# A hybrid encoder block on one core: x2 transposed and split once for both feed-forward chunks, and a planner with a larger reserve per hand-over

## The chip, the cores and the metric

The kernel runs on 1 core of one Trainium2 chip. Time is device microseconds of one execution, and the comparison is between medians of several executions. One execution was also recorded by the hardware profiler; its engines are PE (TensorE, with PEld for its weight loads), DVE (VectorE), ACT (ScalarE), POOL (GpSimd) and SP (SyncE, which issues the DMAs).

## The reference

One encoder layer on 256 tokens of width 2048, in float32, with one final RMSNorm:

```
x = x + W_out [ MLA(h) || DiffAttn(h) ],   h = RMSNorm(x)
x = x + CrossAttn(RMSNorm(x), RMSNorm(mem))        (256 memory tokens, 4 heads)
hf = rms_norm(x, g_ffn)                            # x * rsqrt(mean(x*x) + 1e-6) * g
x = x + (silu(hf @ w_gate) * (hf @ w_up)) @ w_down # w_gate, w_up: 2048 x 5632
return rms_norm(x, g_final)
```

The change is in the third line's `hf`, which the kernel calls x2, and in the first 512 of the 5632 hidden columns.

## The kernel before, in words

**Arithmetic.** TensorE multiplies float32r operands. A value v is held as two halves, h = the rounded copy (a CAST on ACT) and l = v - h (a TENSOR_TENSOR subtract on DVE); a product is three matmuls, h·h, h·l and l·h. `split_into` makes both halves, of weights and of activations alike, so each weight megabyte that arrives (`wraw`) costs ACT two casts and DVE two subtracts of 128x1024.

**Two forms of product.** `project` takes one 512-column chunk: for each of 16 K tiles, 2 token tiles, 3 matmuls of 128x512. `wide_project` takes 1024 columns as a sum over 8 K pairs. A pair of kind "P" is plain: 2 K tiles x 2 token tiles x 2 column halves x 3 = 24 matmuls. A pair of kind "W" uses Winograd's form of Strassen's 2x2 product: 7 block products x 3 = 21 matmuls, at the price of sums. The weights' sums (`tsum`) are one DVE add of 128x1024 and two of 128x512 per pair, and 3.5 instead of 2 subtracts of 1024 columns; the activations' sums are made once by `summed_pair` (4 adds of 128x128, and the forms' splits of 256, 256 and 512 columns). At the end of a wide product `leave` takes the four summed banks out of PSUM (1 ACT copy, 4 DVE operations of 128x512), and `join` adds the four plain banks (4 DVE operations).

**The feed-forward part.** Column block 0 (512 columns) is the narrow chunk, the other 5120 are five wide chunks. After the output projection of cross attention (`w_xo`, 4 column blocks `oc`), each block of x2 is added to the residual (`xres`), transposed on PE, multiplied by g_ffn (`x2T_f`) and split into `x2T`. The narrow chunk uses `x2T` without 1/rms in two `project` calls, gate and up, and multiplies by 1/rms (`rstdf`, tile `x2Tr`) afterwards. Between the two, `normalized_pairs` puts 1/rms into a row (`rb`, two transposes `rps`, `rrow`), multiplies the four `x2T_f` tiles of 128x1024 by it, and splits them a second time, into 4 plain pairs (`x2n`) and 4 summed ones (`forms`). Wide chunks use those. A wide chunk is a gate product, Silu on ACT, an up product, h = up * silu(gate) on DVE, transposes, `hT`, and after every one or two chunks a down product into `xres`.

**What sets the order.** Nothing is issued as it is written: class `Plan` records every operation with its needs and a cost in microseconds, and emits each engine's instructions in an order of its own. A first pass fixes the order of the matmuls; two more passes give each other operation a due time (`wanted`), going back from its readers, and each engine takes the earliest due among what can begin soon. Before the change the step from a reader to what it waits for is the operation's latency plus `HANDOVER` = 0.06 us. All instructions are issued by one recording helper, so they carry one line in the profile (L225 before, L227 in the change): groups are told apart by their tiles.

**Buffers that bind.** `wp` holds 3 raw weight tiles (`wraw`, 1 MB each) and 4 pairs of split halves (`wh`, `wl`). PSUM has 4 accumulator banks and 4 for everything else, and the two sets change places at the end of each wide product.

Of the kernel before, what the change touches and what calls it, by code (L numbers as in the profile page):

```python
# [178 lines left out]
class Plan:  # L179


    HANDOVER, CHOICE = 0.06, 0.3
    BEGUN = {"tensor": 0.6, "vector": 0.8, "scalar": 0.7, "sync": 0.7, "gpsimd": 0.3}

    def __init__(self, tc):
# [59 lines left out]
    def cost(self, engine, method, out, ins, kw):  # L245
        if method == "dma_start":
            size = max(x.cols() for x in out + ins) * 512
            return {"gpsimd": 0.55, "sync": 0.45, "scalar": 0.45}[engine], 2.0 + size / 375e3, size / 381e3
        n = max([x.cols() for x in out[:1]] + ([x.cols() for x in ins[:1]] if "reduce" in method else []))
        in_psum = bool(ins) and ins[0].tile.whole  # L250
        if engine == "tensor":
            t = 0.108 if method == "transpose" else 0.0134 + n / 2400
            return t, t + 0.14, 0.0
        if engine == "gpsimd":
            if method in ("memset", "affine_select", "tensor_copy"):
                t = 0.1 + n * 1.2e-3
            else:
                t = 0.59 if n == 1 else 0.7 if n == 2 else 1.0
            return t, t + 0.03, 0.0
        if engine == "vector":  # L260
            if n <= 16 and "reduce" not in method:
                t = 0.08
            elif method == "scalar_tensor_tensor":
                t = 0.127 + n * 1.05e-3
            elif method == "tensor_scalar":
                t = 0.129 + n * 1.035e-3 if in_psum else n / 960
            elif method == "tensor_tensor_reduce":
                t = 0.145 + n / 960
# [124 lines left out]
    def emit(self, rounds=2):  # L393
        self.order = self.ops
        self.link()
        starts, ended, order = self.run(None, None, False)
        opens = {}
        for o in order:
            for h in o.tiles:
                if h.old is None:  # L400
                    continue
                if h not in opens:
                    opens[h] = done = Op("none", 0.0, 0.0, None)
                    done.number = o.number
# [12 lines left out]
        for n in range(rounds):
            chain = sorted((o for o in self.order if o.engine == "tensor" and not o.free), key=lambda o: starts[o])
            wanted = {}
            for o in reversed(self.order):  # L420
                wanted[o] = starts[o] if o.engine == "tensor" and not o.free else ended
                for x, waits in o.then:
                    wanted[o] = min(wanted[o], wanted[x] - (o.lag + self.HANDOVER if waits else 0.0))
            starts, ended, self.order = self.run(chain, wanted, n == rounds - 1)
            self.log.append(ended)
            self.final = starts
        for p in reversed(self.pools):
            if not p.closed:
                p.shut()
# [17 lines left out]
def encoder_block(tc: tile.TileContext, a, out):  # L447
# [422 lines left out]
    def transposed(dst, src, tt, n, gain=None, raw=None):  # L870
# [5 lines left out]
        if gain is not None:  # L876
# [1 line left out]
            nc.vector.tensor_tensor(out=g[:, :n, :], in0=pv, in1=gain.unsqueeze(2).to_broadcast([P, n, P]),  # L878
                                    op=ALU.mult)
            pv = g[:, :n, :]  # L880
        split_into(dst[:, :n, tt * P:(tt + 1) * P], pv)

    def rms_rows(c, src, tt, width, n, name):

# [321 lines left out]
    for half in range(2):  # L1206
        heads_out(xoT[:, 2 * half:2 * half + 2, :], [pxT[half][:, 0:2, :], pxT[half][:, 2:4, :]], xv, 2 * half)

    x2raw, x2p = [], []
    x2ss = small.tile([P, NT, 4], F32, name="x2ss", tag="x2ss", bufs=1)  # L1210
    for oc in range(4):
        accs = project(lambda kt: xoT[:, kt, :], [a["w_xo"][oc, 0]])
        x2p.append(act_tile(name="x2T"))
        x2raw.append(act.tile([P, 4, S], F32, name="x2T_f", tag="act"))
        for tt in range(NT):
            xs = x_res[tt][:, oc * 512:(oc + 1) * 512]
            nc.vector.tensor_tensor(out=xs, in0=xs, in1=accs[tt], op=ALU.add)
            column_T(x2p[oc], oc, tt, g_f, x2ss, x2raw[oc])
    rstdf = rstd_of_sums(x2ss, "x2T")

    def x2T(kt):
        return x2p[kt // 4][:, kt % 4, :]
    wsum = plan.pool("wsum", 1, closes=[soft, early])
    sum_pool.append(wsum)
    nat_pool[:] = wsum, 5


    def normalized_pairs():

        rb = nat("rb")  # L1230
        rps = ps_tile("rps")
        for tt in range(NT):
            nc.vector.tensor_copy(out=rb[:, tt * P:(tt + 1) * P], in_=rstdf[:, tt:tt + 1].to_broadcast([P, P]))
            nc.tensor.transpose(out=rps[:, tt * P:(tt + 1) * P], in_=rb[:, tt * P:(tt + 1) * P], identity=ident)
        rrow = nat("rrow")
        nc.scalar.copy(out=rrow[:, :S], in_=rps[:, :S])
        for xr in x2raw:
            nc.vector.tensor_tensor(out=xr, in0=xr, in1=rrow[:, :S].unsqueeze(1).to_broadcast([P, 4, S]), op=ALU.mult)
        pairs = []
        t, n = None, 4  # L1240
        for i, kind in enumerate(GU_KINDS):
            xr = x2raw[i // 2][:, i % 2 * 2:i % 2 * 2 + 2, :]
            if kind == "P":
                if n == 4 and "P" in GU_KINDS[i + 1:]:
                    t, n = act_tile(name="x2n"), 0
                elif n == 4:
                    t = Split(*[wsum.tile([P, 2, S], F32R, name="odd" + x, tag="odd" + x, bufs=1) for x in "hl"])
                    n = 0
                split_into(t[:, n:n + 2, :], xr)
                pairs.append(Pair(t[:, n:n + 2, :]))  # L1250
                n += 2
            else:
                pairs.append(summed_pair(xr[:, :, :P], xr[:, :, P:]))
        return pairs

    def narrow_chunk(c):

        ga = project(x2T, [a["w_gate0"][0, i] for i in range(4)])
        xn = normalized_pairs()
        ua = project(x2T, [a["w_up0"][0, i] for i in range(4)])  # L1260
        t = act_tile(name="hT")
        for tt in range(NT):
            r = rstdf[:, tt:tt + 1]
            sg = nat("sg")
            nc.scalar.activation(sg, ga[tt], AF.Silu, scale=r)
            h = nat("h")
            nc.vector.scalar_tensor_tensor(out=h, in0=ua[tt], scalar=r, in1=sg, op0=ALU.mult, op1=ALU.mult)
            transposed(t, h, tt, 4)
        return [Pair(t[:, 0:2, :]), Pair(t[:, 2:4, :])], xn

    def wide_chunk(c, kinds):

        g = wide_result(xn, a["w_gate"][c], G_ORDER, GU_KINDS)
        for oc in range(2):
            for tt in range(NT):
                nc.scalar.activation(g[tt][:, oc, :], g[tt][:, oc, :], AF.Silu)
        u = wide_result(xn, a["w_up"][c], U_ORDER, GU_KINDS)
        for oc in range(2):
# [31 lines left out]
    for gi, (chunks, order) in enumerate(groups):  # L1310
        hp = []
        if gi == 0:
            hp, xn = narrow_chunk(0)
            plan.strict = True
        for c in chunks:
            hp += wide_chunk(c, DN_KINDS[pair0 + len(hp):])
# [93 lines left out]
def _lay_out(i):  # L1410
# [29 lines left out]
        "w_xk": _pieces(i["w_xk"][0])[0],  # L1440
        "w_xv": _pieces(i["w_xv"][0])[0],
        "w_xo": _pieces(i["w_xo"][0]),
        "w_gate0": _pieces(i["w_gate"][0][:, :512]),
        "w_up0": _pieces(i["w_up"][0][:, :512]),
        "w_gate": _pairs(i["w_gate"][0][:, 512:], GU_KINDS),
        "w_up": _pairs(i["w_up"][0][:, 512:], GU_KINDS),
        "w_dn": np.concatenate([_pairs(i["w_down"][0][:, :1024], DN_KINDS), _pairs(i["w_down"][0][:, 1024:], DN_LAST)]),
# [20 lines left out]
```

## Time and profile before

| | us |
|---|---|
| median of 3 runs | 1146.52 (1145.23 to 1147.33) |
| the profiled execution | 1146.09 |
| its span in the profile | 1144.3 |
| PE busy in the span | 1128.8 (99%), 5360 matmuls |
| DVE busy | 1016.5 (89%) |
| ACT busy | 695.1 (61%) |
| POOL busy | 57.7 (5%) |
| weights and inputs read | 219.11 MB, 193 GB/s over the span |

The span is what the profile shows between the first and the last instruction; 1.8 us of the execution lie outside it. A matmul's record is longer than the distance between two of them (389 ns against some 227 ns), so PE's busy share says little on whether it waits: waits are read from the list of waits, and PE's work is counted in matmuls. The feed-forward part starts at about 416 us and ends with the span. The times on a row of the timeline are start and duration in us; a bracket at its end names the idle time before it and what ended that.

### The profile page before, as it was taken

The numbers are of one execution on the slowest core, as the hardware profiler recorded it, in microseconds if no ns is written. First come the engines' busy times: TensorE is split into PE (matmuls) and PEld (weight loads), VectorE is DVE, ScalarE is ACT, GpSimd is POOL, SyncE is SP. The second block draws the span as 40 slices with busy tenths as digits, with TensorE's granted clock in tenths as the row PEclk, the third lists the DMA queues.
The fourth block names the chain that finished last, engine by engine and source line by source line (L and its number), as shares of the span: only waits on it lengthen the run. The fifth ranks groups of instructions, "written<-read, shape, count | busy, mean of one in ns | idle before, by whom it ended". The sixth has DMA issues, their size and how long they took to land.

```text
span 1144.3 us, 14653 instructions
## 1 busy us (share of the span) xinstructions
PE 1128.8 (99%) x5360; PEld 938.8 (82%) x5360; DVE 1016.5 (89%) x1378; ACT 695.1 (61%) x999; POOL 57.7 (5%) x75
## 2 busy tenths in 40 slices
PE   9999999999999999999999999999999999999997
PEld 7889888888888888887878888888788888888776
DVE  6688778678987776999999999999999999999995
ACT  6656455467676555756575565666655665756762
POOL 5820000010000000000000000000000000000000
PEclk9999999999999999999999999999999999999999
DMA  9643444546654444445555566456455554556453
GB/s 355 251 151 125 147 147 151 203 164 242 252 213 173 151 170 166 176 184 201 210 180 219 193 215 218 169 203 220 179 192 215 206 201 181 215 212 236 165 192 121
DMA packets 35496, 222.16 MB, mean 194 GB/s; under 512 B 4320, under 2 KB 5600, under 8 KB 11104
## 3 DMA queue, kind: packets, MB, share of 16 engines
q1 hardware_dynamic: 33696, 216.60, 52.9%
q0 software_dynamic: 864, 3.15, 0.8%
q10 hardware_dynamic: 864, 1.47, 0.4%
q8 instruction: 42, 0.69, 0.2%
q14 instruction: 30, 0.25, 0.1%
HBM read 219.11 MB, written 2.10 MB: 193 GB/s over the span
## 4 chain that ended last, share of the span: by engine, by line
PE 80%; DVE 10%; POOL 3%; issue 2%; DMA 2%; ACT 2%; SPq 0%; POOLq 0%; DVEq 0%; ACTq 0%
PE acc L225 62%; PE q L225 13%; DVE wl L225 4%; PE pt L225 2%; PE psc L225 1%; DVE tsum L225 1%; POOL prod L225 1%; PE qT L225 1%; POOL ang L225 1%; DVE res L225 1%; POOL turns L225 1%; DVE forms_l L225 1%; PE po L225 1%; DMA wraw<-in_w_dn 1%; DVE nm L225 1%
## 5 line engine op out<-in xcount | busy, mean ns | idle before, releaser
L225 ACT CAST wh<-wraw 128x1024 fp32r<-128x1024 f32 (+2 forms) x401 | 387.3, 977 | 224.8 <-PE acc L225 178.5
L225 DVE TENSOR_TENSOR wl<-wraw,wh 128x1024 fp32r<-128x1024 f32 (+2 forms) x401 | 447.7, 1130 | 83.1 <-ACT wh L225 82.0
L225 ACT CAST wh<-tsum 128x1024 fp32r<-128x1024 f32 (+1 forms) x118 | 119.6, 1017 | 127.2 <-DVE tsum L225 77.0
L225 DVE TENSOR_TENSOR wl<-tsum,wh 128x1024 fp32r<-128x1024 f32 (+1 forms) x118 | 138.1, 1174 | 7.7 <-PE acc L225 4.3
L225 PE MATMUL acc<-wh,x2n_h 128*128 128x512 f32 x320 | 124.6, 389 | 0.0
L225 PE MATMUL acc<-wh,x2n_l 128*128 128x512 f32 x320 | 124.6, 389 | 0.0
L225 PE MATMUL q<-wh,forms_h 128*128 128x512 f32 x231 | 91.2, 395 | 0.0
L225 PE MATMUL q<-wh,forms_l 128*128 128x512 f32 x231 | 90.0, 390 | 0.0
L225 PE MATMUL acc<-wh,x0T_h 128*128 128x512 f32 x224 | 88.2, 395 | 0.1
L225 PE MATMUL acc<-wl,x0T_h 128*128 128x512 f32 x224 | 88.1, 394 | 0.0
L225 PE MATMUL acc<-wh,x0T_l 128*128 128x512 f32 x224 | 87.8, 393 | 0.0
L225 PE MATMUL acc<-wl,x2n_h 128*128 128x512 f32 x320 | 86.1, 390 | 0.0
L225 PE MATMUL q<-wl,forms_h 128*128 128x512 f32 x231 | 81.0, 392 | 1.2 <-DVE wl L225 1.2
L225 DVE TENSOR_TENSOR tsum<-tsum,wraw 128x512 f32<-128x512 f32 x118 | 80.8, 684 | 0.8
L225 PE MATMUL acc<-wh,hT_l 128*128 128x512 f32 x188 | 73.8, 393 | 1.2 <-DVE hT_l L225 1.1
L225 PE MATMUL acc<-wh,forms_l 128*128 128x512 f32 x192 | 74.9, 390 | 0.0
L225 PE MATMUL acc<-wh,forms_h 128*128 128x512 f32 x192 | 74.9, 390 | 0.0
L225 DVE TENSOR_TENSOR tsum<-wraw 128x1024 f32<-128x1024 f32 (+1 forms) x64 | 72.3, 1135 | 1.9 <-DMA wraw<-in_w_out 1.0
L225 PE MATMUL acc<-wh,hT_h 128*128 128x512 f32 x188 | 73.4, 390 | 0.0
L225 PE MATMUL acc<-wl,forms_h 128*128 128x512 f32 x192 | 73.0, 390 | 0.0
L225 PEld LDWEIGHTS acc<-wh,x2n_l 128*128 128x128 f32 x320 | 60.1, 188 | 12.5
L225 PEld LDWEIGHTS acc<-wh,x2n_h 128*128 128x128 f32 x320 | 60.1, 188 | 12.4
(377 smaller groups left out, 2147.7 us busy)
## 6 DMA issues: line engine op xcount, KB each, us to landing
wraw<-in_w_gate SPq DMA_DIRECT2D x44, 1024.0 KB, 4.8
wraw<-in_w_up SPq DMA_DIRECT2D x44, 1024.0 KB, 4.8
wraw<-in_w_dn SPq DMA_DIRECT2D x41, 1024.0 KB, 4.8
wraw<-in_w_in SPq DMA_DIRECT2D x24, 1024.0 KB, 4.9
wraw<-in_w_out SPq DMA_DIRECT2D x16, 1024.0 KB, 4.9
wraw<-in_w_in_lat SPq DMA_DIRECT2D x5, 832.0 KB, 7.4
wraw<-in_w_xk SPq DMA_DIRECT2D x4, 1024.0 KB, 5.7
wraw<-in_w_xq SPq DMA_DIRECT2D x4, 1024.0 KB, 4.8
```

The lines of the kernel that those rows point to most:

```text
L225: getattr(getattr(self.tc.nc, engine), method)(*[made(x) for x in args], **{k: made(x) for k, x in kw.items()})
```

## The change

The x2 pairs are made once, as the blocks of x2 come: `transposed(None, ...)` now only multiplies by g_ffn into `raw` (`x2T_f`), and each of its two pairs is split as plain or as summed, without 1/rms. The narrow and the wide chunks share these pairs. 1/rms goes into Silu's scale and into the multiplication by up, for all chunks. `normalized_pairs` is gone. The narrow gate and up become one wide product of 1024 columns (512 of gate, 512 of up; weights `w_gu0`), with pairs 2 and 4 summed and the other six plain. In the planner, due times go back by the latency plus `MARGIN` = 0.4 us instead of 0.06; `HANDOVER` stays 0.06 where the passes place operations in time. POOL's small operations are costed at 1.0 or 1.2 us instead of 0.59 to 1.0.

```diff
+NARROW_KINDS, NARROW_ORDER = "PPWPWPPP", (0, 1, 3, 2, 5, 4, 6, 7)
 class Plan:
-    HANDOVER, CHOICE = 0.06, 0.3
+    HANDOVER, MARGIN, CHOICE = 0.06, 0.4, 0.3
 ...
-                t = 0.59 if n == 1 else 0.7 if n == 2 else 1.0
+                t = 1.0 if n <= 2 else 1.2
 ...
                 for x, waits in o.then:
-                    wanted[o] = min(wanted[o], wanted[x] - (o.lag + self.HANDOVER if waits else 0.0))
+                    wanted[o] = min(wanted[o], wanted[x] - (o.lag + self.MARGIN if waits else 0.0))
 ...
-        split_into(dst[:, :n, tt * P:(tt + 1) * P], pv)
+        if dst is not None:
+            split_into(dst[:, :n, tt * P:(tt + 1) * P], pv)
 ...
-    x2raw, x2p = [], []
+    x2_pairs = []
     x2ss = small.tile([P, NT, 4], F32, name="x2ss", tag="x2ss", bufs=1)
+    plain = []
     for oc in range(4):
         accs = project(lambda kt: xoT[:, kt, :], [a["w_xo"][oc, 0]])
-        x2p.append(act_tile(name="x2T"))
-        x2raw.append(act.tile([P, 4, S], F32, name="x2T_f", tag="act"))
+        raw = act.tile([P, 4, S], F32, name="x2T_f", tag="act")
         for tt in range(NT):
             xs = x_res[tt][:, oc * 512:(oc + 1) * 512]
             nc.vector.tensor_tensor(out=xs, in0=xs, in1=accs[tt], op=ALU.add)
-            column_T(x2p[oc], oc, tt, g_f, x2ss, x2raw[oc])
+            transposed(None, xs, tt, 4, g_f[:, 4 * oc:4 * oc + 4], raw)
+            meansq(xs, x2ss[:, tt, oc:oc + 1], 512, D)
+        for n in range(2):
+            rows = raw[:, 2 * n:2 * n + 2, :]
+            if GU_KINDS[2 * oc + n] == "W":
+                x2_pairs.append(summed_pair(rows[:, :, :P], rows[:, :, P:]))
+                continue
 ...
+            split_into(plain[0], rows)
+            x2_pairs.append(Pair(plain.pop(0)))
 ...
-    def normalized_pairs():
 ...
     def narrow_chunk(c):
-        ga = project(x2T, [a["w_gate0"][0, i] for i in range(4)])
-        xn = normalized_pairs()
-        ua = project(x2T, [a["w_up0"][0, i] for i in range(4)])
+        both = wide_result(x2_pairs, a["w_gu0"], NARROW_ORDER, NARROW_KINDS)
         t = act_tile(name="hT")
         for tt in range(NT):
             r = rstdf[:, tt:tt + 1]
 ...
-            nc.scalar.activation(sg, ga[tt], AF.Silu, scale=r)
-            h = nat("h")
-            nc.vector.scalar_tensor_tensor(out=h, in0=ua[tt], scalar=r, in1=sg, op0=ALU.mult, op1=ALU.mult)
+            g, h = both[tt][:, 0, :], both[tt][:, 1, :]
+            nc.scalar.activation(g, g, AF.Silu, scale=r)
+            nc.vector.scalar_tensor_tensor(out=h, in0=h, scalar=r, in1=g, op0=ALU.mult, op1=ALU.mult)
             transposed(t, h, tt, 4)
 ...
     def wide_chunk(c, kinds):
-                nc.scalar.activation(g[tt][:, oc, :], g[tt][:, oc, :], AF.Silu)
+                nc.scalar.activation(g[tt][:, oc, :], g[tt][:, oc, :], AF.Silu, scale=rstdf[:, tt:tt + 1])
 ...
-                nc.vector.tensor_tensor(out=h, in0=h, in1=g[tt][:, oc, :], op=ALU.mult)
+                nc.vector.scalar_tensor_tensor(out=h, in0=h, scalar=rstdf[:, tt:tt + 1], in1=g[tt][:, oc, :],
+                                               op0=ALU.mult, op1=ALU.mult)
```

The planner's numbers move instructions everywhere, though PE's order ahead of the feed-forward part stays the same but for some transposes. Three places follow on which the prediction rests. The first is PE near 58 us, where the normalized latents `cq` and `ckv` and the rotated key `kr` are transposed into PSUM (`pt`) in the middle of a projection from `x0T`; before:

```order
L225 MATMUL pt<-ident,cq 128x128 x8
L225 MATMUL pt<-ident,ckv 128x128 x2
L225 MATMUL pt<-ident,kr 128x128 x2
L225 MATMUL acc<-wh,x0T_h 128x512
L225 MATMUL pt<-ident,ckv 128x128 x2
L225 MATMUL acc<-wl,x0T_h 128x512
```

And in the change:

```order
L227 MATMUL pt<-ident,cq 128x128 x8
L227 MATMUL pt<-ident,ckv 128x128 x4
L227 MATMUL acc<-wh,x0T_h 128x512
L227 MATMUL acc<-wl,x0T_h 128x512
L227 MATMUL acc<-wh,x0T_l 128x512
L227 MATMUL acc<-wh,x0T_h 128x512
```

Four banks now take two `cq` and two `ckv` tiles; the `kr` transposes, which stood third, stand 17 matmuls behind them.

The second is DVE where two wide chunks end and their down product begins (twice in the program: near 808 and near 1060 us). `hT_l` is the low half of the first down pairs' activations, `wl`, `tsum` and `forms_l` belong to weights and sums. Before:

```order
L225 TENSOR_TENSOR forms_l<-res_6585,forms_h 128x256 x2
L225 TENSOR_TENSOR wl<-wraw,wh 128x1024 x2
L225 TENSOR_TENSOR tsum<-wraw 128x1024
L225 TENSOR_TENSOR forms_l<-sums,forms_h 128x512
L225 TENSOR_TENSOR hT_l<-res_7259,hT_h 128x4x128
L225 TENSOR_TENSOR wl<-wraw,wh 128x1024
L225 TENSOR_TENSOR hT_l<-res_7287,hT_h 128x4x128
```

In the change:

```order
L227 TENSOR_TENSOR forms_l<-res_6579,forms_h 128x256 x2
L227 TENSOR_TENSOR wl<-wraw,wh 128x1024 x2
L227 TENSOR_TENSOR tsum<-wraw 128x1024
L227 TENSOR_TENSOR hT_l<-res_7246,hT_h 128x4x128
L227 TENSOR_TENSOR hT_l<-res_7281,hT_h 128x4x128
L227 SCALAR_TENSOR_TENSOR res_7246<-res_7246,x2Tr,res_6912 128x512
L227 TENSOR_TENSOR wl<-wraw,wh 128x1024
```

A `forms_l` of 512 columns and a `wl` of 1024 have gone from ahead of the second `hT_l` to behind it.

The third is DVE at the start of the narrow chunk's first summed pair. Before, the stretch held plain weights and the multiplication by `rrow`:

```order
L225 COPY rb<-x2Tr 128x128 x2
L225 TENSOR_TENSOR wl<-wraw,wh 128x1024 x6
L225 TENSOR_TENSOR x2T_f<-x2T_f,rrow 128x1024 x2
L225 TENSOR_TENSOR wl<-wraw,wh 128x1024
L225 TENSOR_TENSOR x2T_f<-x2T_f,rrow 128x1024
```

In the change it holds the forms of the summed pairs (`forms_l<-sums` x4 for all four) and the first weight sums; `wl_4519<-tsum` is the half of the third and fourth sum, `wl<-tsum` behind it that of the first two:

```order
L227 TENSOR_TENSOR wl<-wraw,wh 128x1024
L227 TENSOR_TENSOR forms_l<-sums,forms_h 128x512 x4
L227 TENSOR_TENSOR wl<-wraw,wh 128x1024
L227 TENSOR_TENSOR tsum<-wraw 128x1024
L227 TENSOR_TENSOR tsum<-tsum,wraw 128x512
L227 TENSOR_TENSOR wl<-wraw,wh 128x1024
L227 TENSOR_TENSOR tsum<-tsum,wraw 128x512
L227 TENSOR_TENSOR wl<-wraw,wh 128x512
L227 TENSOR_TENSOR forms_l<-x2T_f,forms_h 128x256
L227 TENSOR_TENSOR x2T_l<-x2T_f,x2T_h 128x512
L227 TENSOR_TENSOR wl_4519<-tsum,wh_4504 128x1024
L227 TENSOR_TENSOR wl<-tsum,wh 128x1024
```

So the splits and sums of x2 stand ahead of the narrow product's first summed pair, where before they were spread from there to the end of the first wide gate.

More of the change, by code (lines that the diff above doesn't have):

```diff
@@ L1217, in encoder_block @@
             nc.vector.tensor_tensor(out=xs, in0=xs, in1=accs[tt], op=ALU.add)
-            column_T(x2p[oc], oc, tt, g_f, x2ss, x2raw[oc])
+            transposed(None, xs, tt, 4, g_f[:, 4 * oc:4 * oc + 4], raw)
[5 more added lines that the diff above has]
+                continue
+            if not plain:
+                t = act_tile(name="x2T")
+                plain = [t[:, 0:2, :], t[:, 2:4, :]]
+            split_into(plain[0], rows)
+            x2_pairs.append(Pair(plain.pop(0)))
     rstdf = rstd_of_sums(x2ss, "x2T")
-    def x2T(kt):
-        return x2p[kt // 4][:, kt % 4, :]
     wsum = plan.pool("wsum", 1, closes=[soft, early])
@@ L1225, in encoder_block @@
     nat_pool[:] = wsum, 5
-    def normalized_pairs():
[L1230 to L1254, printed above, removed]
     def narrow_chunk(c):
-        ga = project(x2T, [a["w_gate0"][0, i] for i in range(4)])
-        xn = normalized_pairs()
-        ua = project(x2T, [a["w_up0"][0, i] for i in range(4)])
+        both = wide_result(x2_pairs, a["w_gu0"], NARROW_ORDER, NARROW_KINDS)
         t = act_tile(name="hT")
@@ L1263, in narrow_chunk @@
             r = rstdf[:, tt:tt + 1]
-            sg = nat("sg")
-            nc.scalar.activation(sg, ga[tt], AF.Silu, scale=r)
-            h = nat("h")
-            nc.vector.scalar_tensor_tensor(out=h, in0=ua[tt], scalar=r, in1=sg, op0=ALU.mult, op1=ALU.mult)
+            g, h = both[tt][:, 0, :], both[tt][:, 1, :]
+            nc.scalar.activation(g, g, AF.Silu, scale=r)
+            nc.vector.scalar_tensor_tensor(out=h, in0=h, scalar=r, in1=g, op0=ALU.mult, op1=ALU.mult)
             transposed(t, h, tt, 4)
-        return [Pair(t[:, 0:2, :]), Pair(t[:, 2:4, :])], xn
+        return [Pair(t[:, 0:2, :]), Pair(t[:, 2:4, :])]
     def wide_chunk(c, kinds):
-        g = wide_result(xn, a["w_gate"][c], G_ORDER, GU_KINDS)
+        g = wide_result(x2_pairs, a["w_gate"][c], G_ORDER, GU_KINDS)
         for oc in range(2):
             for tt in range(NT):
-                nc.scalar.activation(g[tt][:, oc, :], g[tt][:, oc, :], AF.Silu)
-        u = wide_result(xn, a["w_up"][c], U_ORDER, GU_KINDS)
+                nc.scalar.activation(g[tt][:, oc, :], g[tt][:, oc, :], AF.Silu, scale=rstdf[:, tt:tt + 1])
+        u = wide_result(x2_pairs, a["w_up"][c], U_ORDER, GU_KINDS)
         for oc in range(2):
@@ L1312, in encoder_block @@
         if gi == 0:
-            hp, xn = narrow_chunk(0)
+            hp = narrow_chunk(0)
             plan.strict = True
@@ L1442, in _lay_out @@
         "w_xo": _pieces(i["w_xo"][0]),
-        "w_gate0": _pieces(i["w_gate"][0][:, :512]),
-        "w_up0": _pieces(i["w_up"][0][:, :512]),
+        "w_gu0": _pairs(np.concatenate([i["w_gate"][0][:, :512], i["w_up"][0][:, :512]], axis=1), NARROW_KINDS)[0],
         "w_gate": _pairs(i["w_gate"][0][:, 512:], GU_KINDS),
```

## The prediction

> **What bounds the kernel now.** I began with the busy shares, went on to the list of PE's waits, then to the stretches of the feed-forward part, and last to single rows around each wait.
>
> ```profile
> PE 1128.8 (99%) x5360; PEld 938.8 (82%) x5360; DVE 1016.5 (89%) x1378; ACT 695.1 (61%) x999; POOL 57.7 (5%) x75
> ```
>
> The list of PE's waits (total, times, longest):
>
> ```profile
> PE pt L225 <- DVE gT L225: 1.9, 1, 1.9
> PE wps L225 <- DVE warm L225: 1.2, 1, 1.2
> PE q L225 <- DVE wl L225: 1.2, 2, 0.9
> PE acc L225 <- DVE hT_l L225: 1.1, 2, 0.6
> PE pdt L225 <- DVE on L225: 1.1, 2, 0.7
> PE pt L225 <- DVE h L225: 0.5, 1, 0.5
> ```
>
> PE works nearly always: these lines come to 7.0 us, 1.2 of them (`warm`) ahead of the first product, and below them only three waits of 0.2 are left. So time can come from two places only, PE's own work and these waits; and new time can only come from an engine that makes PE wait. Every line but `warm` names DVE. How full DVE is, the stretches show (length, then busy us and count of PE, PEld, DVE, ACT and POOL, PE's granted clock, DMA share, GB/s): x2's transposes, the narrow chunk, the first wide chunk, the group of two, and the last chunks.
>
> ```profile
> 416.00:440.00 24.00, 24.00 (x123) 20.01 (x122) 21.89 (x30) 16.35 (x30) 0.00 (x0) 1.00 0.39 135
> 440.00:484.00 44.00, 43.53 (x198) 35.78 (x197) 33.43 (x48) 27.41 (x39) 0.69 (x1) 1.00 0.54 189
> 484.00:594.00 110.00, 108.84 (x484) 88.45 (x482) 109.52 (x142) 70.50 (x88) 0.00 (x0) 1.00 0.52 188
> 594.00:810.00 216.00, 215.39 (x961) 177.61 (x959) 211.12 (x246) 131.03 (x155) 0.00 (x0) 1.00 0.58 207
> 810.00:1104.00 294.00, 293.32 (x1304) 240.69 (x1305) 287.77 (x344) 186.39 (x228) 1.10 (x2) 1.00 0.56 199
> ```
>
> From 484 to 1104 DVE is busy 608.4 of 620 us: PE sets the pace with DVE a step behind, and work added there would be paid in full. In the narrow stretch DVE idles 10.6 of 44 us, and before it 2.1 of 24. That is all the room that x2 and the narrow chunk offer.
>
> **Prices.** The chain of waits gives PE's pitch, DVE's timeline gives that of its operations:
>
> ```profile
> 615.05 5.67 PE acc L225 x25
> 356.01 1.75 PE pt L225 x16
> 597.20 3.48 DVE L225 TENSOR_TENSOR wl<-wraw,wh 128x1024 fp32r<-128x1024 f32 x3
> 565.55 1.28 DVE L225 TENSOR_TENSOR res<-acc,res 128x512 f32<-128x512 f32 x2
> 800.16 0.75 DVE L225 TENSOR_TENSOR forms_l<-res,forms_h 128x256 fp32r<-128x256 f32 x2
> 798.22 0.48 DVE L225 TENSOR_TENSOR sums<-res 128x128 f32<-128x128 f32 x2
> ```
>
> A matmul of 512 columns costs 5.67/25 = 0.227 us, a transpose 1.75/16 = 0.11. DVE's records overlap a little, so of a run the first is taken off: 1024 columns cost about 1.13, 512 columns 0.60, 256 columns 0.33, 128 columns 0.20.
>
> **The change part by part.**
>
> *A, PE's work.* Narrow gate and up were 2 x 96 = 192 matmuls; they become 6 x 24 + 2 x 21 = 186, and the two `rps` transposes go: 6 x 0.227 + 2 x 0.11 = **-1.6**. That is certain, since PE's clock is 1.00 and no wait covers it.
>
> [...]
>
> *DVE's work.* Eight splits of 512 (4.8), four multiplications by `rrow` (4.6) and two `rb` (0.3) go: -9.7. The narrow weights' halves grow from 16 to 19 units of 1024 columns (+3.4), with two sets of `tsum` (2 x (1.13 + 2 x 0.60) = 4.7) and `leave` and `join` (8 x 0.60 = 4.8). The multiplication by 1/rms inside h is priced by its nearest rows:
>
> ```profile
> L225 DVE TENSOR_TENSOR res<-res,res 128x512 f32<-128x512 f32 x20 | 13.7, 683 | 0.1
> L225 DVE SCALAR_TENSOR_TENSOR h<-acc,x2Tr,sg 128x512 f32<-128x512 f32 x2 | 1.4, 740 | 0.0
> ```
>
> It costs 740 - 683 = 57 ns more, 20 times: 1.1. So DVE gains 14.0 and loses 9.7: +4.3 of work. It is hidden by the 12.7 us that DVE idles from 416 to 484; with that cover gone it would cost PE up to 4.3. The 1.1 of it that falls into the wide chunks lies under DVE's 11.6 idle us there. ACT is busy 61%: its changes cost nothing, which its own idle hides.
>
> *B, the wait at 61.76.*
>
> ```profile
> 57.79 0.56 POOL L225 TENSOR_TENSOR rkv<-rkv,mhalf 128x1 f32<-128x1 f32 x1
> 58.39 0.35 DVE L225 TENSOR_SCALAR ckv<-ckv,rkv 128x256 f32<-128x256 f32 x1 [1.05 <-POOL rkv L225]
> 58.66 2.44 DVE L225 TENSOR_TENSOR wl<-wraw,wh 128x1024 fp32r<-128x1024 f32 x2
> 61.02 0.68 DVE L225 TENSOR_TENSOR gT<-pt,gains 128x512 f32<-128x512 f32 x1
> 61.76 0.33 PE L225 MATMUL pt<-ident,ckv 128*128 128x128 f32 x1 [1.93 <-DVE gT L225]
> ```
>
> The last `ckv` transposes need a bank that `gT` empties, and `gT` stands on DVE behind two `wl`. In the change the two `ckv` tiles fit into the free banks; `kr`, which took one, comes 17 matmuls (3.9 us) later, and one `wl` stands ahead of `gT`, not two. What is late next is `kr`, by at most a few tenths. **-1.9** (bounds: 0, if `kr` waits as long; -1.9).
>
> *C, the waits for `on`.*
>
> ```profile
> 175.64 1.22 DVE L225 TENSOR_TENSOR wl<-wraw,wh 128x1024 fp32r<-128x1024 f32 x1
> 175.82 1.62 POOL L225 TENSOR_TENSOR rd<-rd,mhalf 128x2 f32<-128x2 f32 x1 [91.27 <-DVE rd L225]
> 178.11 0.30 PE L225 MATMUL pdt<-ident,on 128*128 128x128 f32 x1 [0.72 <-DVE on L225]
> 178.51 0.70 POOL L225 TENSOR_TENSOR rd<-rd,mhalf 128x2 f32<-128x2 f32 x1 [1.06 <-DVE rd L225]
> 251.68 0.30 PE L225 MATMUL pdt<-ident,on 128*128 128x128 f32 x1 [0.36 <-DVE on L225]
> ```
>
> POOL's power took 1.62 us beside a `wl`, 0.70 alone, and the planner counts 0.7; in the change 1.0. The first transposes then stand two matmuls later (0.45) and the second place has both powers ahead. I take **-0.9** (bounds 0 and -1.1).
>
> [...]
>
> *D, the narrow h, and E, the waits for `wl`.*
>
> ```profile
> 482.06 0.33 PE L225 MATMUL pt<-ident,h 128*128 128x128 f32 x1 [0.47 <-DVE h L225]
> 517.42 0.50 PE L225 MATMUL q<-wl,forms_h 128*128 128x512 f32 x1 [0.22 <-DVE wl L225]
> 559.37 0.69 DVE L225 TENSOR_TENSOR res<-q,res 128x512 f32<-128x512 f32 x1
> 593.29 1.22 DVE L225 TENSOR_TENSOR wl<-wraw,wh 128x1024 fp32r<-128x1024 f32 x1
> 593.43 0.50 PE L225 MATMUL q<-wl,forms_h 128*128 128x512 f32 x1 [0.94 <-DVE wl L225]
> ```
>
> At 482 h came straight from the last product; now a gate product leads, and the transposes have the first wide gate's matmuls to stand behind: **-0.5** (0 and -0.5). The wait at 517 stands behind the forms of x2, which the change has made by then. That at 593 ends a run of DVE from `leave` to a weight sum's half: 593.29 - 559.37 = 33.9 us. In the change a `wl` of 1024 and forms have left that run, some 2.4 us by the prices: the half comes earlier than PE asks. **-1.2** (0 and -1.2).
>
> *F, the waits for `hT_l`.*
>
> ```profile
> 807.52 0.68 DVE L225 TENSOR_TENSOR hT_l<-res,hT_h 128x512 fp32r<-128x512 f32 x1
> 808.12 1.22 DVE L225 TENSOR_TENSOR wl<-wraw,wh 128x1024 fp32r<-128x1024 f32 x1
> 809.25 0.68 DVE L225 TENSOR_TENSOR hT_l<-res,hT_h 128x512 fp32r<-128x512 f32 x1
> 809.99 0.50 PE L225 MATMUL acc<-wh,hT_l 128*128 128x512 f32 x1 [0.55 <-DVE hT_l L225]
> ```
>
> The `forms_l` of 512 and the `wl` that leave the place ahead of the second `hT_l` make it 1.13 + 0.60 = 1.7 us earlier, against a wait of 0.6; less 0.2 for four dearer multiplications. It goes at 808 and at 1060. The `wl` behind is late next, with a pair of matmuls (24 x 0.227 = 5.4 us) ahead of its use. **-1.1** (0 and -1.1).
>
> *G, new waits.* At the narrow chunk's first summed pair, PE has from the end of the first `w_xo` product 154 matmuls and 32 transposes, 154 x 0.227 + 32 x 0.11 = 38.5 us, until it needs the low half of the first two sums. DVE has to do by then, in 1024 columns, 12 `wl` (two of them of sums) and a `tsum` (13 x 1.13 = 14.7), in 512 columns 8 `xres`, 8 `x2T_f`, 4 `x2T_l`, 4 `forms_l`, 2 `tsum` and a `wl` (27 x 0.60 = 16.2), 2 of 256 (0.7) and 16 sums (3.2): 34.8. That leaves 3.7 us for hand-overs; DVE idled 2.1 of 24 us in such work, 3.4 in 38.5. So it just fits. A DVE that is late here is late for `wl`, and PE stands with all its later matmuls behind that one. With the tenths of `kr` I take **+1.0** (bounds 0 and +3.4).
>
> Sum: -1.6 - 1.9 - 0.9 - 0.5 - 1.2 - 1.1 + 1.0 = **-6.2**. The profiled execution took 1146.09 (span 1144.3 and 1.8 outside), 0.4 below the median, so it becomes 1139.9, and the median 1146.5 - 6.2 = **1140.3**.
>
> **The rivals.**
>
> *The waits only move.* For it: 110 us in which DVE idles half a microsecond (484 to 594), so what leaves one place may be due at the next, and the reserve of 0.4 adds no capacity. Against: B and C lie where DVE isn't full, and F's order is plain. Only A stays: 1146.5 - 1.6 = 1144.9.
>
> *VectorE late at the first summed pair (slower).* The 16 sums, 8 forms of 256 and 4 of 512, 3.2 + 2.6 + 2.4 = 8.2 us, are due before pair 2 now; before, they had 75 us, into the first wide gate. If hand-overs take DVE over PE's 38.5 us point by that much, PE pays it, as nothing later gives it back, and with DVE late the waits of D, E and F stay: 1146.5 - 1.6 - 2.8 (B, C) + 8.2 = 1150.3. It is slower from the point where the lateness passes 4.4, where PE's gain and B and C are used up. For it: G's fit is close. Against: 3.7 us of slack must go first, so for the full price hand-overs would need about 12 us where 3.4 are to be expected.
>
> *All waits go.* The reserve of 0.4 is larger than every small wait on the list, so `warm` (1.2) and the three of 0.2 could go too, and G stay at 0: 1140.3 - 1.2 - 0.6 - 1.0 = 1137.5. For it: POOL's dearer costs move its operations forward everywhere. Against: `warm` stands at the program's start, where nothing can be put ahead of it.
>
> **How the numbers follow.** Main case 0.60, moved waits 0.19, late VectorE 0.10, all waits gone 0.11. A difference of 0.2% (2.3 us) is about what this measurement can tell. Faster: the main case, all waits gone, and 0.03 of the moved waits (a wait or two may still go), 0.74; same 0.16; slower 0.10. The main case's own range is 1139 to 1142.7: below, G at 0 and C at its lower bound (1139.1); above, G at 3.4 (1142.7), or C and E at 0 (1142.4). The whole range, 1137 to 1145, takes in the cases on both sides of it, from all waits gone to moved waits, and leaves out the late VectorE.
>
> **What would show it.** A: 8 records fewer on PE. B: no `gT` in the list of PE's waits, and none above 0.3 for `kr`. C: no `on`. D, E, F: `h`, `wl`, `hT_l` gone. G: a wait for `wl` at the first `forms_h` after 440 of under 1 us, while DVE is over 95% busy from 416 to there. It is wrong if that wait is above 4, or if `hT_l` or `wl` waits stand in the wide chunks again with a sum like the old one.

## The result, and the profile after

The change takes 1137.09 us (median of 4 runs, 1136.84 to 1137.43) against 1146.22 before: a ratio of 0.992, 95% interval 0.9903 to 0.9937, so 9.1 us faster. It was predicted at 1140.3, within 1137.0 to 1145.0: the direction was right and the time lies at the very bottom of the range. Half again as much was gained as the sum held (-6.2), and the question of the experiments is which terms were too small, and whether the parts of the change that were named for them are the ones that earned them.

Busy shares and PE's list of waits after:

```profile
PE 1124.2 (99%) x5352; PEld 938.8 (83%) x5352; DVE 1020.6 (90%) x1382; ACT 698.9 (62%) x995; POOL 59.1 (5%) x75
PE q L227 <- ACT res L227: 1.4, 2, 0.7
PE wps L227 <- DVE warm L227: 1.2, 1, 1.2
PE po L227 <- ACT e L227: 0.5, 1, 0.5
PE po L227 <- ACT val_h L227: 0.2, 1, 0.2
```

Eight records fewer on PE, and `gT`, `wl`, `hT_l`, `on` and `h` are off the list. Two new entries stand there, both for ACT: its copy `res` (twice 0.7, near 716 and 967 us) and `e` (0.5, at 111). The list shrank from 7.6 us to 3.3, which with PE's -1.6 explains 5.9 of the 9.0 us by which the profiled span went from 1144.3 to 1135.3.

Where the rest is, the starts of the same matmul in the two traces tell (worked out from the two traces; from 493 us on the matmuls are counted from the end, since eight are gone in the narrow chunk):

```
place (time before)                     before   change   difference
first pt of cq                           58.12    58.35     +0.24
first acc from cqT                       67.51    65.63     -1.88
first pt of dn                          115.48   114.17     -1.31
first pod                               172.12   170.15     -1.97
first q of the output projection        269.19   266.15     -3.04
first po of cross attention             407.79   404.18     -3.60
2881st from the end, first wide gate    493.24   487.60     -5.64
2581st, end of the first wide up        562.08   555.60     -6.48
2401st, first pair's down product       602.87   594.98     -7.89
1861st, second half of the up at 716    723.68   716.55     -7.14
1561st, end of the third up             791.68   784.57     -7.12
1441st, down product at 808             818.38   810.03     -8.35
 721st, up at 980                       980.26   972.65     -7.60
 301st, down product at 1060           1074.98  1066.11     -8.87
last                                   1136.41  1127.44     -8.97
```

Most of the large steps lie where the prediction put a term, and most of those are larger than their entry on the list of waits; the steps up to 115, to 172, to 408, at 716 and at 980 lie elsewhere. The place at 808 shows why the list falls short. PE's timeline before, around the waits for `hT_l`:

```profile
807.80 0.40 PE L225 MATMUL acc<-wh,hT_h 128*128 128x512 f32 x1
808.25 0.50 PE L225 MATMUL acc<-wh,hT_l 128*128 128x512 f32 x1
...
809.05 0.40 PE L225 MATMUL acc<-wh,hT_h 128*128 128x512 f32 x1
809.99 0.50 PE L225 MATMUL acc<-wh,hT_l 128*128 128x512 f32 x1 [0.55 <-DVE hT_l L225]
810.33 0.40 PE L225 MATMUL acc<-wh,hT_h 128*128 128x512 f32 x1
```

A matmul's record lasts 0.40 us, but the next one normally starts 0.227 after it. So the bracket, which counts from the end of a record, leaves out the first 0.17 us of every pause: from 809.05 to 809.99 PE lost 0.94 - 0.227 = 0.71, not 0.55, and from 807.80 to 808.25 it lost 0.22 and the list shows nothing at all. Here that is 0.93 lost beside 0.55 listed. The matmul behind each pause is late as well: 810.33 is 0.34 after 809.99, 0.11 more than usual, and 808.59 is as late after 808.25. That makes 1.15; the measured gain at this place is 1.23. The same holds at 593 (592.10 to 593.43 is 1.33, so 1.10 lost, 0.94 listed). Added up in this way over the whole traces, from start to start and against the usual distance of each form of matmul, PE lost 15.2 us before and 7.7 in the change. These 7.5 and PE's -1.6 account for the 9.0.

VectorE after, in the narrow chunk's stretch, with the columns as in the prediction:

```profile
440.00:484.00 44.00, 43.97 (x199) 36.18 (x198) 43.55 (x58) 26.75 (x31) 0.69 (x1) 1.00 0.51 173
```

From 440 to 484 DVE is now busy 43.55 of 44 us (33.43 before), and the list has no wait of PE there (from start to start there is one, of 0.19, at 478.69). How close that is, the next rows show: the two halves of the first sums on DVE, and on PE the first readers of each.

```profile
449.11 1.22 DVE L227 TENSOR_TENSOR wl<-tsum,wh 128x1024 fp32r<-128x1024 f32 x1
449.11 2.35 DVE L227 TENSOR_TENSOR wl<-tsum,wh 128x1024 fp32r<-128x1024 f32 x2
450.39 0.39 PE L227 MATMUL q<-wl,forms_h 128*128 128x512 f32 x1
451.75 0.39 PE L227 MATMUL q<-wl,forms_h 128*128 128x512 f32 x1
```

The first half is ready at 450.33, 0.06 us ahead of its reader, the second at 451.46, 0.29 ahead.

### The profile page after: what moved, and what is told of

Read it like the earlier page. It is cut to its first block, busy times and chain, and to the rows that moved or that the text cites. A ratio compares the mean times of both kernels' runs of the same rounds, so it can differ in the third digit from the quotient of the medians.

```text
span 1135.3 us, 14659 instructions
## 1 busy us (share of the span) xinstructions
PE 1124.2 (99%) x5352; PEld 938.8 (83%) x5352; DVE 1020.6 (90%) x1382; ACT 698.9 (62%) x995; POOL 59.1 (5%) x75
## 4 chain that ended last, share of the span: by engine, by line
PE 92%; DVE 5%; issue 1%; ACT 1%; POOL 0%; POOLq 0%; DVEq 0%; ACTq 0%
PE acc L227 70%; PE q L227 13%; DVE wl L227 2%; PE pt L227 2%; PE psc L227 2%; PE acckv L227 1%; PE qT L227 1%; PE po L227 1%; DVE tsum L227 1%; DVE res L227 1%; PE kT L227 1%; PE ppt L227 1%; ACT wh L227 0%; PE wps L227 0%; DVE forms_l L227 0%
## 5 line engine op out<-in xcount | busy, mean ns | idle before, releaser
L227 ACT CAST wh<-tsum 128x1024 fp32r<-128x1024 f32 (+1 forms) x122 | 123.9, 1017 | 104.0 <-PE acc L227 68.5
L227 PE MATMUL acc<-wh,x2T_l 128*128 128x512 f32 x352 | 137.3, 390 | 0.0
L227 PE MATMUL acc<-wh,x2T_h 128*128 128x512 f32 x352 | 137.1, 390 | 0.0
L227 PE MATMUL acc<-wl,x2T_h 128*128 128x512 f32 x352 | 94.5, 389 | 0.0
L227 PE MATMUL acc<-wh,forms_l 128*128 128x512 f32 x214 | 83.6, 391 | 0.0
L227 PE MATMUL acc<-wh,forms_h 128*128 128x512 f32 x214 | 83.5, 390 | 0.0
L227 PE MATMUL acc<-wl,forms_h 128*128 128x512 f32 x214 | 79.4, 389 | 0.0
L227 PEld LDWEIGHTS acc<-wl,x2T_h 128*128 128x128 f32 x352 | 66.1, 188 | 13.7
L227 PEld LDWEIGHTS acc<-wh,x2T_l 128*128 128x128 f32 x352 | 66.1, 188 | 13.6
L227 PEld LDWEIGHTS acc<-wh,x2T_h 128*128 128x128 f32 x352 | 66.1, 188 | 13.6
```

The source lines that it names most:

```text
L227: getattr(getattr(self.tc.nc, engine), method)(*[made(x) for x in args], **{k: made(x) for k, x in kw.items()})
```

## The experiments

Two theories stood against each other. S: the waits for `h`, `wl` and `hT_l` went because the structure (split once, one narrow product) took work off VectorE at the right places. R: they went because of the planner's reserve of 0.4 us. POOL's costs were taken by both to be what removed `gT` and `on`.

### The parts of the change one by one

The structure alone (the edit is against the change):

```diff
-    HANDOVER, MARGIN, CHOICE = 0.06, 0.4, 0.3
+    HANDOVER, MARGIN, CHOICE = 0.06, 0.06, 0.3
 ...
-                t = 1.0 if n <= 2 else 1.2
+                t = 0.59 if n == 1 else 0.7 if n == 2 else 1.0
```

> The change's split-once x2, its narrow product and 1/rms in Silu and h, with the planner's numbers of before (reserve 0.06, POOL's small operations at 0.59 to 1.0). Theory S (the waits for h, wl and hT_l go because the structure takes work off VectorE behind the narrow chunk; the waits for gT and on go by POOL's dearer costs): PE's work -1.6, h -0.5, wl -2.2, hT_l -2.5, so 1146.2 - 6.8 = 1139.4, with the waits for gT (1.9) and on (1.1) still on the list. Theory R (the reserve is what removes wl and hT_l): only PE's work and h go, 1146.2 - 2.1 = 1144.1, and wl and hT_l stay on the list with about 2.3 together.

Measured: 1145.26, ratio 0.9989 (0.9979 to 0.9998). Theory S falls: its 1139.4 is 6 us off. Its list of PE's waits:

```profile
PE q L227 <- ACT res L227: 2.0, 2, 1.0
PE pt L227 <- DVE gT L227: 1.9, 1, 1.9
PE acc L227 <- DVE hT_l L227: 1.4, 2, 0.7
...
PE pdt L227 <- DVE on L227: 1.1, 2, 0.7
...
PE q L227 <- DVE wl L227: 0.5, 1, 0.5
```

`h` is gone, and of the two waits for `wl` the one at 517; the one at 593 shrinks to 0.5. `hT_l` is there, somewhat larger than before on the list, somewhat smaller from start to start (0.97 against 1.16 at each place). The new waits for `res` are there too: they come with the structure, and the reserve makes them smaller (0.7 against 1.0).

The median of 1145.26 lies where none of the ten runs does. Five took 1143.59 to 1144.54 us, with a mean granted clock of 0.998 or 0.999 on PE, and five 1145.98 to 1146.66, with 0.997. The profiled one is of the second group, and 1.6 us of it are matmuls at a lower clock behind the pause at 62 (see the last section). The kernel before has both groups too: of its 19 runs in this series 14 lie from 1145.31 to 1146.59 at 0.998 or 0.999 and five from 1147.64 to 1148.36 at 0.996 or 0.997. Between the groups of the higher clock the structure takes the median from 1146.1 to 1143.7, which is near theory R's 1144.1.

The planner's numbers alone, put into the kernel before:

```diff
-    HANDOVER, CHOICE = 0.06, 0.3
+    HANDOVER, MARGIN, CHOICE = 0.06, 0.4, 0.3
 ...
-                t = 0.59 if n == 1 else 0.7 if n == 2 else 1.0
+                t = 1.0 if n <= 2 else 1.2
 ...
-                    wanted[o] = min(wanted[o], wanted[x] - (o.lag + self.HANDOVER if waits else 0.0))
+                    wanted[o] = min(wanted[o], wanted[x] - (o.lag + self.MARGIN if waits else 0.0))
```

> The kernel before with the reserve of 0.4 and POOL's costs of 1.0 and 1.2, nothing else. Theory S: the waits for gT and on go (-3.1), wl and hT_l stay near 2.3 on the list, and the new waits for ACT's res at about 720 and 970 are there (up to +1.5): 1143 to 1144.6. Theory R: gT, on, wl and hT_l all go (-7.8), 1138.4 to 1140.

Measured: 1139.56, ratio 0.9938 (0.9923 to 0.9952). That is theory R: three quarters of the gain without touching the arithmetic.

```profile
PE q L225 <- ACT res L225: 1.4, 2, 0.7
...
PE pt L225 <- DVE h L225: 0.5, 1, 0.5
PE po L225 <- ACT e L225: 0.5, 1, 0.5
...
PE po L225 <- ACT val_h L225: 0.2, 1, 0.2
```

Neither `wl` nor `hT_l` is left, with the old structure; `h` is, as it must be. The waits for `res` and `e` appear here without the structure, so either part by itself is enough to bring `res`, and `e` belongs to the reserve.

POOL's costs alone, in the kernel before:

```diff
-                t = 0.59 if n == 1 else 0.7 if n == 2 else 1.0
+                t = 1.0 if n <= 2 else 1.2
```

> The kernel before with POOL's costs of 1.0 and 1.2 alone. By both theories the waits for gT and on go and all others stay: 1146.2 - 3.1 = 1143.1. If the reserve was needed for them, one or both are still on the list and the time is 1144 to 1146.

Measured: 1144.04, ratio 0.9976 (0.9967 to 0.9986), at the lower end of the second case. `gT` is off the list, `on` only halved:

```profile
PE q L225 <- DVE wl L225: 1.3, 2, 0.9
...
PE acc L225 <- DVE hT_l L225: 1.1, 2, 0.6
PE pdt L225 <- DVE on L225: 0.6, 2, 0.4
```

The change with the small reserve (against the change, as all edits from here on):

```diff
-    HANDOVER, MARGIN, CHOICE = 0.06, 0.4, 0.3
+    HANDOVER, MARGIN, CHOICE = 0.06, 0.06, 0.3
```

> The change with the reserve back at 0.06, POOL's costs kept. Theory S: PE's work, h, wl, hT_l, gT and on all gone, 1146.2 - 9.9 = 1136.3, and if the new waits for ACT's res (1.4 on the list of the change) come from the reserve, this is as fast as the change or faster. Theory R: wl and hT_l back on the list, 1137.1 + 4.7 = 1141.8.

Measured: 1141.59, ratio 0.9956 (0.9939 to 0.9972), theory R's number. `hT_l` (1.4), `wl` (0.6), `on` (0.6) and `res` (2.0) are on its list, and a wait of 1.0 for ACT's `wh` near 9 us, at the start of the program, where some of these kernels have one (0.6 with the structure alone) and others none.

The change with POOL's old costs:

```diff
-                t = 1.0 if n <= 2 else 1.2
+                t = 0.59 if n == 1 else 0.7 if n == 2 else 1.0
```

> The change with POOL's small operations costed as before (0.59 to 1.0), the reserve of 0.4 kept. If the wait for gT goes by POOL's costs alone, it is back with 1.9 on the list (2.2 from start to start), 1137.1 + 2.2 = 1139.3, and the waits for on stay gone if the reserve covers them, else 1140.3. If the reserve is enough for both: 1137.1.

Measured: 1139.31 (1138.05 to 1139.83), ratio 0.9932 (0.992 to 0.9945).

```profile
PE pt L227 <- DVE gT L227: 0.9, 1, 0.9
PE pdt L227 <- DVE rd L227: 0.6, 1, 0.6
...
PE pdt L227 <- DVE on L227: 0.3, 1, 0.3
```

Without POOL's costs the reserve halves `gT`, and most of the waits around `on` stay (0.9 for `rd` and `on`, against 1.1 before). POOL's costs by themselves had removed `gT` and halved `on`. So `gT` needs only POOL's costs; `on` needs both.

The change itself, measured once more:

> The change as it is, for a comparison on one chip: 1137.1, within 0.5.

Measured: 1137.16 (1137.0 to 1137.29), ratio 0.9915 (0.9902 to 0.9929).

So, with POOL's costs in place, the reserve takes 1144.04 to 1139.56 on the old structure and 1141.59 to 1137.1 on the new: -4.5 both times. POOL's costs take 1146.3 to 1144.0 without the other two and 1139.3 to 1137.1 with them: -2.2 both times. The structure, with POOL's costs, takes 1144.0 to 1141.6 and 1139.6 to 1137.1: -2.5 both times, near the terms A and D (-2.1). The three come to -9.2, the whole gain, and half of it is the reserve's. From the kernel before to the structure alone it is 1.0 by the medians, and from there POOL's costs earn 3.7 and the reserve 6.0, as if the parts did not add. By the runs of the higher clock alone (1146.1 and 1143.7) these become 2.4, 2.1 and 4.4: they add. Two things were not run: the reserve without the other two, and the two halves of the structure (x2 split once, the narrow product with sums) each by itself.

### How large a reserve

```diff
-    HANDOVER, MARGIN, CHOICE = 0.06, 0.4, 0.3
+    HANDOVER, MARGIN, CHOICE = 0.06, 0.6, 0.3
```

> The change with the reserve at 0.6. In the change, after the first product of an up pair, the first matmul on a sum's half (q) stands right behind the last transposes and waits for ACT's copy res of them, 0.7 twice. Here four matmuls (0.9) stand between. Theory P (that wait is a matter of place, and a larger reserve moves the place): both go and nothing else comes, 1137.1 - 1.5 = 1135.6. Theory Q (VectorE and ACT have no time left, the pause turns up elsewhere): 1137 and as much waiting on the list as the change (3.3).

Measured: 1138.98 (1138.1 to 1139.57), ratio 0.9931 (0.9914 to 0.9948). Theory P was right on the place (no wait for `res`) and wrong on the time: as theory Q has it, a pause turned up elsewhere, in the down products, near 823 and 1074. Q's own number, 1137, was 2 us too low.

```profile
PE q L227 <- DVE forms_l L227: 1.3, 2, 0.6
```

With 0.8 in that line:

> The change with the reserve at 0.8, twice its value. Theory P: as with 0.6, 1135.6 or a few tenths around it. Theory Q: due times that are too early fill the four buffers of split weights sooner, VectorE does work early that isn't needed and late work that is, and the waits for wl come back: 1137.5 to 1140.

Measured: 1154.9 (1151.56 to 1155.7), ratio 1.0063 (1.0044 to 1.0081): slower than the kernel before.

```profile
PE acc L227 <- DVE wl L227: 9.9, 6, 3.0
...
PE acc L227 <- DVE left L227: 1.2, 1, 1.2
```

Theory Q's sign and its waits for `wl` are there, but its 1137.5 to 1140 was far too mild: the longest of the six last 3 us, and some cost more than they last (1.6 us more behind the one of 2.98, see the last section). That early work fills the four pairs of buffers is what Q argued; no run changed their number, so that cause is not shown.

### How full VectorE is in the narrow chunk

The first summed pair early:

```diff
-NARROW_KINDS, NARROW_ORDER = "PPWPWPPP", (0, 1, 3, 2, 5, 4, 6, 7)
+NARROW_KINDS, NARROW_ORDER = "PPWPWPPP", (0, 2, 1, 3, 5, 4, 6, 7)
```

> The change with the narrow chunk's first summed pair second instead of fourth: PE needs the half of its sums 48 matmuls (10.9 us) earlier, and four wl (4.5) can move behind it. Theory G (the prediction's count of VectorE's work up to that half, 3.7 us of slack): 3.7 - 10.9 + 4.5 = -2.7, so PE waits for a wl or for the forms near 435 us by 2.7 or more: 1139.8 to 1142. Theory H (the reserve and the rest of VectorE's idle time leave far more room than counted): 1137 to 1138, no such wait.

Measured: 1136.92 (1136.7 to 1137.45), ratio 0.9912 (0.9897 to 0.9927), the same as the change. No wait came. But this does not show that there was room: the planner's first pass chooses the matmuls' order, and it took only the products on unsummed weights early. DVE's and PE's timelines of this kernel:

```profile
434.60 0.39 PE L227 MATMUL q<-wh,forms_h 128*128 128x512 f32 x1
...
440.08 0.39 PE L227 MATMUL acc<-wh,forms_l 128*128 128x512 f32 x1
447.28 1.23 DVE L227 TENSOR_TENSOR wl<-tsum,wh 128x1024 fp32r<-128x1024 f32 x1
449.40 0.39 PE L227 MATMUL q<-wl,forms_h 128*128 128x512 f32 x1
```

From 434.6 to 440.1 a few matmuls of the pair run; the first half of a sum is made at 447.28, and its product follows at 449.40. In the change that was 450.39: the need moved by 1.0 us, not by 10.9. As a test of the slack the run fails.

A third summed pair, which adds real work:

```diff
-NARROW_KINDS, NARROW_ORDER = "PPWPWPPP", (0, 1, 3, 2, 5, 4, 6, 7)
+NARROW_KINDS, NARROW_ORDER = "PPWPWPWP", (0, 1, 3, 2, 5, 4, 7, 6)
```

> The change with a third summed pair in the narrow product (pair 6, seventh and eighth exchanged): three matmuls less (-0.7), and VectorE has 1.5 halves of 1024 columns and a set of sums more, 1.7 + 2.3 = 4.0. From 440 to 484 VectorE is busy 43.55 of 44 in the change. Theory G (no room): PE waits for wl at that pair or in the wide gate behind, 1137.1 - 0.7 + 2 to 4 = 1138.5 to 1140.5. Theory H (there is room, work moves ahead): 1136.4.

Measured: 1141.03 (1140.42 to 1141.82), ratio 0.9948 (0.9933 to 0.9962). Three matmuls less, 3.9 us more: VectorE has no room there. The wait is in another place than expected, not for `wl` but for the accumulator banks that DVE empties at the product's end (`res`), and it shows at 475 to 478. The three pauses come to 2.7 us from start to start; behind them PE's clock falls for a while (0.70 from 478 to 482, last section), which brings the time above theory G's 1140.5.

```profile
PE acc L227 <- DVE res L227: 2.2, 3, 1.2
474.00:478.00 4.00, 2.27 (x8) 0.98 (x7) 3.96 (x8) 1.50 (x2) 0.00 (x0) 1.00 0.71 252
```

### The new pause at 716 and 967

Two more kernels tried to take it away by its place in PE's order.

```diff
-    def emit(self, rounds=2):
+    def emit(self, rounds=4):
```

> The change with four planning passes that go back for due times instead of two, the reserve at 0.4. The last transposes of the first up product of a pair of chunks stand three matmuls ahead of the q that waits for their copy (one ahead of it in the change, none between), so by place alone (theory P) the pause of 0.88 at 716 and 967 shrinks by two matmuls, 0.45 each: 1137.1 - 0.9 = 1136.2. Theory Q (the pause only moves, as with the reserve of 0.6): 1137.1 or more.

```diff
-    HANDOVER, MARGIN, CHOICE = 0.06, 0.4, 0.3
+    HANDOVER, MARGIN, CHOICE = 0.06, 0.35, 0.3
 ...
-    def emit(self, rounds=2):
+    def emit(self, rounds=3):
```

> The change with a reserve of 0.35 and three passes: one matmul between the last transposes and q. Theory P: 0.23 less at each of the two places, 1136.6. Theory Q: 1137.1 or more. If the smaller reserve brings back the waits for hT_l or wl, 1138 and above.

Measured: 1136.92 (1136.51 to 1137.36) and 1137.07 (1136.73 to 1137.4), ratios 0.9912 (0.9896 to 0.9927) and 0.9914 (0.9901 to 0.9928): both the same as the change. With four passes there are two matmuls between the transposes and `q`, and the pause is not shorter. ACT's and PE's timelines of that kernel, and for comparison those of the change:

```profile
714.93 0.60 PE L227 MATMUL pt<-ident,res 128*128 128x128 f32 x4
714.25 1.99 ACT L227 CAST wh<-wraw 128x1024 fp32r<-128x1024 f32 x2
716.15 0.57 ACT L227 COPY res<-pt 128x512 f32<-128x512 f32 x1
716.77 0.50 PE L227 MATMUL q<-wh,forms_h 128*128 128x512 f32 x1 [0.78 <-ACT res L227]
```

```profile
708.77 0.60 PE L227 MATMUL pt<-ident,res 128*128 128x128 f32 x4
709.40 0.59 ACT L227 COPY res<-pt 128x512 f32<-128x512 f32 x1 [2.26 <-PE pt L227]
...
714.67 0.60 PE L227 MATMUL pt<-ident,res 128*128 128x128 f32 x4
714.38 1.06 ACT L227 CAST wh<-wraw 128x1024 fp32r<-128x1024 f32 x1
715.33 0.60 ACT L227 COPY res<-pt 128x512 f32<-128x512 f32 x1
715.98 0.50 PE L227 MATMUL q<-wh,forms_h 128*128 128x512 f32 x1 [0.71 <-ACT res L227]
```

In the change ACT's copy begins 0.66 us after the first transpose. That is hardly later than where ACT stood idle (709.40, 0.63 after 708.77), so its casts cost nothing there: the pause is the way from PE through ACT and back, 1.31 us from 714.67 to 715.98, with no matmul between the transposes and `q`. With four passes two matmuls stand between, but the copy begins only 1.22 us after the first transpose, behind two casts, so the casts now hold it by some 0.6. What the place gains, ACT's order gives back. (That kernel's list also has 0.9 for ACT's `wh` near 9 us.) With 0.35, and one matmul between, the pause shrank to 0.4 on the list, and small ones at 388 and 480 took its place. Whether the pause can be removed without a new one stays open; no version tried is measurably faster than the change.

## Why the prediction was right, and where it was not

**Direction and A.** Right. Eight records are gone, and the stretch that holds A and D moved by 5.64 - 3.60 = 2.04; the sum had 1.6 + 0.5. VectorE's work grew by 4.1 us (1016.5 to 1020.6) where 4.3 were counted.

**B, `gT`.** Right: -2.1 between 58 and 66 us against -1.9. `gT` now follows one `wl`, and `kr` came without a wait on the list. POOL's costs alone are enough for it; with the reserve and without them 0.9 stays.

**C, `on`.** Right in size: from -1.97 to -3.04, so -1.07 against -0.9. POOL's powers that began beside a `wl` took 1.62 and 1.71 us before (175.82 and 249.30), the two others 0.70 and 0.69. In the change three take 0.69, but the first one still begins beside a `wl` (173.55 to 174.77) and takes as long as before,

```profile
173.72 1.63 POOL L227 TENSOR_TENSOR rd<-rd,mhalf 128x2 f32<-128x2 f32 x1 [91.15 <-DVE rd L227]
```

and PE's transposes begin 2.3 us behind its start, at 176.02, as before (175.82 and 178.11). But two matmuls more now stand ahead of them, so PE works through most of what was a pause, and at 251 nothing is left. The step "POOL's costs do it" was incomplete: with them alone 0.6 of the 1.1 stays.

**D, `h`.** Right: gone from the list with the structure alone. In the change 0.19 of it remains from start to start, of 0.63.

**E, the waits for `wl`, mis-sized and half wrongly explained.** Measured -0.84 from 493 to 562 and -1.41 from 562 to 603, together -2.25 against the -1.2 that the bounds did not let it exceed. For 517 the reason was right (structure alone removes it). For 593 the step "a `wl` of 1024 and forms have left that run" named the work rightly but not what moves it: the structure alone leaves 0.5 on the list, the planner's numbers alone remove it in the old structure, and as POOL's costs alone leave it there, it is the reserve that does.

**F, the waits for `hT_l`, mis-sized.** Measured -1.23 and -1.27 at the two places, -2.5 against -1.1. What moves the operations is the reserve, not the structure: the planner's numbers alone remove these waits, and the change with the small reserve has 1.4 on the list.

For E and F the failed step is that the list's total was taken as the upper bound of the gain. The list leaves out 0.17 us of each pause, every pause shorter than that, and the 0.11 by which the next matmul is late. (That every line of that list but `warm` names DVE is a slip: `warm` does too.)

**G, new waits, wrong in place and half the size.** +1.0 was set for the first summed pair of the narrow chunk and `kr`. There the wait is 0; "it just fits" was literally so, by 0.06 and 0.29 us. The sign given for it, DVE over 95% busy from 416 to there, was missed by a little: 32.22 of 34.40 us, 94%. Instead +0.75 came at 716 and +0.75 at 967, for ACT's `res`, and +0.6 at 111, for `e`. That is +2.1, inside G's bounds of 0 and 3.4, but for another reason. The step that failed is the one that held ACT's changes to cost nothing because ACT is busy 61%: PE's new order puts `q` right behind the transposes, and then the copy's own time counts (0.60 of the 1.31 us from the transposes to `q` at 714.67), however idle ACT is.

**Not foreseen.** -0.56 between 269 and 408 and -0.66 between 115 and 172 us, mostly pauses of 0.3 to 0.4 before `e`, `dn` and `pod` that the list showed with 0.2 or not at all. This is the rival in which all waits go, in part: its 1137.5 came nearest, but `warm` stayed, and its G of 0 was not to be had.

**The number.** That the time still fell into the range is in part luck. E and F were some 2.5 too small and 1.2 was not foreseen; what kept the time from falling below the range is that G was 1.1 too small the other way. Without the pauses at 111, 716 and 967 it would have been about 1135.0.

**The other rivals.** The waits did not merely move (1144.9), except in part, with the new pauses worth some 2.1 us. VectorE late (1150.3) did not occur, but with 1.7 + 2.3 us more work it did, at the end of the product.

## What to carry to other kernels

A list of waits that is counted from record to record sets no upper bound: where records are longer than the pitch (0.40 against 0.227 here), measure pauses from start to start. A planner that places work just in time loses by each hand-over it underrates; a reserve of 0.4 earned half the gain here, and 0.35 with one pass more was as good, but 0.6 gave 1.9 us back and 0.8 all of it and some 8 us more, so it is to be measured, not set generously. An engine that is busy 61% can still be the one that another waits for: a copy between two operations of PE cost its own time (0.60 us) where nothing stood between them, and more where casts stood ahead of it (with four passes it began 1.22 us after the first transpose, instead of 0.66).

## What the runs showed of the hardware

In some places a pause of PE cost more than it lasted. With the reserve of 0.8, PE's timeline and windows of 4 us behind a wait of 2.98 us for `wl`:

```profile
530.28 0.65 PE L227 MATMUL acc<-wl,forms_h 128*128 128x512 f32 x1 [2.98 <-DVE wl L227]
530.74 0.63 PE L227 MATMUL acc<-wh,forms_l 128*128 128x512 f32 x1
531.16 0.63 PE L227 MATMUL q<-wh,forms_h 128*128 128x512 f32 x1
...
533.72 0.47 PE L227 MATMUL acc<-wh,x2T_h 128*128 128x512 f32 x1
526.00:530.00 4.00, 1.31 (x6) 0.75 (x4) 4.00 (x5) 2.91 (x4) 0.00 (x0) 1.00 0.02 4
530.00:534.00 4.00, 3.72 (x9) 2.94 (x10) 3.26 (x5) 1.51 (x2) 0.00 (x0) 0.57 0.82 287
```

The granted clock falls to 0.57 in the second window, and eight matmuls start 0.43 us apart instead of 0.227: 1.6 us more, over 3.4 us. In the same kernel two later waits for `wl` last 2.80 us each, at 767.32 and 1024.03. Only the second is followed by a lower clock:

```profile
768.00:772.00 4.00, 4.00 (x19) 3.27 (x18) 4.00 (x6) 2.32 (x3) 0.00 (x0) 1.00 0.92 379
1024.00:1028.00 4.00, 3.98 (x12) 3.18 (x13) 3.97 (x5) 1.67 (x2) 0.00 (x0) 0.67 0.83 320
```

A slow stretch also followed the three pauses of 0.6 to 1.4 us at the end of the narrow product with three summed pairs (0.70 from 478 to 482), and a pause of 1.9 us in the kernel with the structure alone, while the pause of 1.93 at 61.76 in the kernel before left the clock at 1.00 (62 to 66 us, 1.00). Windows of the two kernels behind the pause at 62:

```profile
62.00:66.00 4.00, 3.74 (x14) 2.98 (x15) 3.91 (x8) 1.76 (x4) 0.66 (x2) 0.68 0.25 103
```

```profile
62.00:66.00 4.00, 4.00 (x21) 3.29 (x20) 3.91 (x8) 2.46 (x6) 0.15 (x1) 1.00 0.24 80
```

The first is the structure alone, the second the kernel before: the same pause, 0.68 and 1.00. What decides between them no run here settles. One execution of each kernel was recorded (of the change two). That the runs of lower mean clock hold such stretches is seen in one of them, that of the structure alone; for the others it is inferred from their clock and their time.
